# Loads of x.T and weights in another order, VectorE turns a second x.T tile, and the first normed x by rows and transposes

## The chip, the cores and the metric

The kernel runs on one core of a Trainium2 chip. The metric is the device time of one execution in microseconds (us). The engines of the core work side by side and wait for each other by semaphores: TensorE (PE in the profile, its weight loads PEld), VectorE (DVE), ScalarE (ACT), GpSimd (POOL) and SyncE (SP), whose queue issues nearly all DMAs here.

## The reference

Two transformer blocks in float32 over a sequence of 256 tokens of width 1024. What matters for the change is the first half layer:

```python
h = rmsnorm(x, norm_gain[0])                       # x * rsqrt(mean(x*x) + eps) * gain
qa, ka, va, qb, kb, vb, qm, gate = split_cols(h @ w_in_even[0], SPLIT_EVEN)
qa = rope_2d(rmsnorm(qa, q_norm_a), ...); ka = rope_2d(rmsnorm(ka, k_norm_a), ...)
ya, yb, ym = global_gqa(qa, ka, va), window_gqa(qb, kb, vb, ...), memory_attn(qm, mk, mv)
x = x + (concat(ya, yb, ym) * silu(gate)) @ w_out_even[0]
```

A second layer with neighborhood attention, a final norm, a hybrid mixer, a cross attention and an MLP follow; the change leaves them alone.

## The kernel before, in words

All products run on TensorE in float32r. Each operand is split into a high part, its value rounded to float32r, and a low part, the rest: three matmuls (high-high, high-low, low-high) give the product. A weight is loaded raw, ScalarE writes its high part (`t_wh`), VectorE its low part (`t_wl`; `split`, line 430). Raw weights have three buffers, the parts four each.

The work is not issued as written. Class `Plan` records every operation; `order` (line 162) then lays them out in time by a cost for each and a priority (place in the program, plus a bias), and the kernel is issued in the order that comes out. A DMA there takes its bytes over a rate, line 227. On the chip each engine runs its own stream strictly in that order.

The first half layer (`layer_even`, line 1008) starts before the norm's factor is known. x.T, the transposed input, is loaded in eight tiles of 128 features by `load_x` (line 392) and multiplied by the gain (`gain_t`, line 519; `t_gh`, high and low). For each of the eight weight tiles of 128 rows ("tile 0" to "tile 7"), `sweep` makes 12 matmuls with the columns of q, k and v of a and v of b (896 columns: 512 in two banks, 384 in two). Since the factor belongs to a token, it is multiplied in afterwards, on the results. The first x.T tile is turned by VectorE, the others by ScalarE.

The other projections want normed x.T. x itself is loaded by rows into two halves of 128 tokens, squared and summed; `rstd` makes the factor r on VectorE and GpSimd. `spread` (line 534) makes a diagonal of it and multiplies it with ones on TensorE, so that each partition holds all factors (`t_y`). Eight multiplies on VectorE (x.T times gain times spread factor, `t_xs`) and `hilo` give the high and low parts `t_hT`. Then come b's key (128 weight columns), the gates of a (two loads of 256 columns), mem-q (two loads), the keys and values of the memory, and so on. Beside them VectorE, ScalarE and GpSimd work on the rope of k and q, whose turned tiles go through TensorE transposes (`t_at<-t_cst,t_p`; `t_cst` holds the identity), and on the gain of the memory (`t_gh<-t_memT`).

Later norms of the kernel go by another way: x by rows times r (`t_xn`, `scaled`, line 644, on VectorE or ScalarE), 16 transposes of 128 x 128 on TensorE, and high and low parts out of PSUM with the gain (`t_mT`; `turns`, line 657).

Before the first data, 24 matmuls on zeros (`t_warm`) keep TensorE busy from 1.19 to 6.4 us.

Of the kernel before, what the change touches and what calls it, by code (L numbers as in the profile page):

```python
# [10 lines left out]
F32 = mybir.dt.float32  # L11
# [5 lines left out]
P = 128  # L17
# [12 lines left out]
class Plan:  # L30
# [131 lines left out]
    def order(self, prio):  # L162
# [37 lines left out]
        while len(seq) < n:  # L200
            best = None
            for e, c in cand.items():
                if not c:
                    continue
                t = max(avail[e][0], min(ready[i] for i in c))
                if best is None or t < best[0]:
                    best = (t, e)
            t, e = best
            c = cand[e]
            i = min((i for i in c if ready[i] <= t), key=lambda i: (prio[i], i))  # L210
            o = ops[i]
            for form in o["forms"]:
                cand[form[0]].remove(i)
            self.form[i] = next(f for f in o["forms"] if f[0] == e)
            start[i] = t
            self.held[i] = why[i] if ready[i] >= avail[e][0] else avail[e][1]
            end[i] = t + self.form[i][4]
            avail[e] = (end[i], i)
            done = end[i]
            if o["bytes"]:  # L220
                if e != "gpsimd":
                    ring[e] = max(ring[e], t) + 450.0
                    avail[e] = (ring[e], i)
                    bus = max(bus, ring[e] + 650.0)
                else:
                    bus = max(bus, end[i] + 650.0)
                bus += o["bytes"] / 358.0
                done = bus + o["after"]
            self.done[i] = done
            seq.append(i)  # L230
            for j, lat in self.next[i]:
                arrive(j, done + (lat if not o["bytes"] else 0.0), i)
            for name in o["uses"]:
                last[name] = max(last[name], (done + 190.0, i))
                left[name] -= 1
                if left[name] == 0:
                    k = self.key[name]
                    heapq.heappush(free[k], last[name] + (self.slot[name],))
                    give(k)
# [68 lines left out]
class Kernel:  # L308
# [59 lines left out]
    def consts(self):  # L368
# [9 lines left out]
        warm = self.base.tile([P, S], F32R, name="warm")  # L378
        nc.vector.memset(warm.bitcast(F32), 0.0)
        self.xT = [self.slot([P, 4, S], "xT", F32) for _ in range(2)]  # L380
        for k, queue in enumerate((nc.sync, nc.scalar)):
            self.load_x(k, 1, queue)
        busy = self.psum("at")
        for _ in range(WARM):
            nc.tensor.matmul(busy[:, 0, :], warm[:, :P], warm, start=True, stop=True)
# [133 lines left out]
    def gain_t(self, src, key, fast=False):  # L519

        nc = self.nc
        f = Halves(lambda: self.slot([P, 2, 2, S], "gh"))

        def turn(k):
            v, g, h, l = src[k // 4][:, k % 4, :], self.gcol(key, k), f(0, k), f(1, k)
            if k == 0 and fast:
                nc.vector.tensor_scalar(h, v, g, None, ALU.mult)
            else:
                nc.scalar.activation(h, v, AF.Copy, scale=g)
            nc.vector.scalar_tensor_tensor(l, v, g, h.bitcast(F32), ALU.mult, ALU.subtract)  # L530

        return f, turn
# [475 lines left out]
    def layer_even(self):  # L1008
# [5 lines left out]
        def columns(k0, parts, raw=None):  # L1014


            if raw is None:
                raw = self.wp.tile([P, 2, 896], F32, tag="raw", name=self.name("raw"), bufs=3)
            for j0, j1, d0, d1 in parts:
                c = d0 if d0 < 768 else d0 + 640  # L1020
                nc.sync.dma_start(raw[:, j0:j1, d0:d1], w_in[(k0 + j0) * P:(k0 + j1) * P, c:c + d1 - d0]
                                  .rearrange("(k p) c -> p k c", p=P))
            return raw
# [11 lines left out]
                             k == 0, k == KT - 1)  # L1035

        for k0 in range(0, KT, 2):
            raw = columns(k0, ((0, 1, 0, 512), (0, 2, 512, 768), (0, 2, 768, 896), (1, 2, 0, 512)) if k0 == 0 else
                          ((0, 2, 0, 768), (0, 2, 768, 896)) if k0 < 6 else ((0, 1, 0, 768), (0, 1, 768, 896)))
            if k0 < 6:  # L1040
                self.load_x(k0 + 2, 2, nc.sync)
            else:
                for t in range(2):
                    nc.ahead = True
                    nc.sync.dma_start(self.x[:, t, :], a["x"][0, t * P:(t + 1) * P])
                    nc.ahead = False
                columns(k0, ((1, 2, 0, 768), (1, 2, 768, 896)), raw)
# [8 lines left out]
        for c in range(2):  # L1056
            squares(c)
        r = self.rstd(ms)
        rb = self.spread(r, self.work("y", [P, S], YB))
        hT = Halves(lambda: self.slot([P, 2, 2, S], "hT"))  # L1060
        for c in range(2):
            t = self.slot([P, 4, S], "xs", F32)
            for k in range(4):
                nc.vector.scalar_tensor_tensor(t[:, k, :], self.xT[c][:, k, :], self.gcol("norm0", 4 * c + k), rb,
                                               ALU.mult, ALU.mult)
            for k in (0, 2):
                self.hilo(*hT.pair(4 * c + k), t[:, k:k + 2])
        nc.bias = 0
        self.sink = self.base.tile([P, 8], F32, name="sink")
        nc.sync.dma_start(self.sink, a["sink_b"].to_broadcast([P, 8]))  # L1070
# [488 lines left out]
```

## Time and profile before

| | |
|---|---|
| median of 3 runs | 773.08 us (772.73 to 773.56) |
| profiled execution | 773.77 us, its span 771.9 us |
| TensorE busy | 760.7 us, 99% of the span |
| VectorE, ScalarE busy | 614.3 us (80%), 529.0 us (69%) |
| chain that ended last | PE 82%, ACT 6%, DVE 6%, DMA 3% |
| granted TensorE clock | 0.997 of full speed over the span |

Matmuls overlap, and their ends are modelled, so a busy TensorE is one that had no long pause, and the pauses are found in the list of waits and in the timeline. All operations are recorded by one helper, so the line in most rows is L284; groups are told apart by tiles: `t_mm` and `t_at` are PSUM banks, `t_raw` a raw weight, `out<-in` says what is written from what. The queue of an engine, which issues its DMAs, has a q behind its name (SPq).

### The profile page before, as it was taken

Reading aid. Unit: us, or ns where it says so; the run is one execution under the profiler, and the core shown is the slowest. Engines: PE = TensorE matmul, PEld = TensorE weight load, DVE = VectorE, ACT = ScalarE, POOL = GpSimd, SP = SyncE. Lnnn points to the kernel's source line nnn. Section 1 sums busy time; section 2 is a strip of 40 time slices with the busy share of each in tenths; the row PEclk is TensorE's granted clock in tenths of the full one; section 3 lists DMA queues with packets and bytes.
Section 4 is the critical chain, followed back from the end, with each engine's and each line's share of the span. In section 5 each row is a group of like instructions: output and inputs, shape, how many; then the busy total and the mean of one; then the engine's idle time right before and its main releaser. Section 6 shows DMA issues by size and latency. Waiting matters only on the chain.

```text
span 771.9 us, 11841 instructions
## 1 busy us (share of the span) xinstructions
PE 760.7 (99%) x4370; PEld 662.6 (86%) x4370; DVE 614.3 (80%) x1136; ACT 529.0 (69%) x1034; POOL 66.6 (9%) x98
## 2 busy tenths in 40 slices
PE   9999999999999999999999999999999999999996
PEld 7898888888888888888888898899988888888885
DVE  5999998988779789979998899886677665555655
ACT  5687986976678678757796788466556765555562
POOL 2140010000001511132001000100000000000000
PEclk9999999999999999999999999999999999999998
DMA  8893555445568854765456644356535665656541
GB/s 315 284 268 111 165 183 177 159 165 164 164 211 250 218 188 144 199 197 193 134 191 194 191 163 156 117 165 219 191 110 164 195 188 167 204 177 209 170 163 55
DMA packets 109145, 140.39 MB, mean 182 GB/s; under 512 B 3744, under 2 KB 80736, under 8 KB 109088
## 3 DMA queue, kind: packets, MB, share of 16 engines
q1 hardware_dynamic: 103184, 131.12, 52.7%
q0 software_dynamic: 5472, 8.10, 4.8%
q8 instruction: 34, 0.56, 0.3%
q10 hardware_dynamic: 432, 0.43, 0.2%
q14 instruction: 23, 0.19, 0.1%
HBM read 134.92 MB, written 1.05 MB: 176 GB/s over the span
## 4 chain that ended last, share of the span: by engine, by line
PE 82%; ACT 6%; DVE 6%; DMA 3%; issue 2%; SPq 0%; POOLq 0%; POOL 0%; ACTq 0%; DVEq 0%
PE t_mm L284 61%; PE t_at L284 21%; DVE t_wl L284 2%; DMA t_raw<-in_w_in_even_dram 2%; ACT t_p L284 2%; ACT t_wh L284 2%; ACT t_y L284 1%; DVE t_y L284 1%; DVE t_p L284 1%; DMA t_xT<-in_x_t_dram 0%; ACT t_ph L284 0%; SPq L284 0%; ACT t_sum L284 0%; DVE t_pl L284 0%; DVE t_tanh L284 0%
## 5 line engine op out<-in xcount | busy, mean ns | idle before, releaser
L284 DVE TENSOR_TENSOR t_wl<-t_raw,t_wh 128x1024 fp32r<-128x1024 f32 (+2 forms) x238 | 288.7, 1217 | 69.9 <-ACT t_wh L284 67.2
L284 ACT ACTIVATE t_wh<-t_raw 128x1024 fp32r<-128x1024 f32 (+2 forms) x238 | 249.7, 1054 | 78.7 <-PE t_mm L284 57.4
L284 PE MATMUL t_mm<-t_mT,t_wh 128*128 128x512 f32 x496 | 179.6, 401 | 0.0
L284 PE MATMUL t_mm<-t_mT,t_wl 128*128 128x256 f32 x496 | 131.0, 283 | 0.0
L284 PE MATMUL t_mm<-t_wh,t_yh 128*128 128x512 f32 (+1 forms) x288 | 113.3, 393 | 0.0
L284 PE MATMUL t_mm<-t_wl,t_yh 128*128 128x512 f32 (+1 forms) x288 | 112.3, 390 | 0.0
L284 PE MATMUL t_mm<-t_wh,t_yl 128*128 128x512 f32 (+1 forms) x288 | 111.9, 391 | 0.0
L284 PEld LDWEIGHTS t_mm<-t_mT,t_wh 128*128 128x128 f32 x496 | 91.0, 188 | 13.4
L284 PEld LDWEIGHTS t_mm<-t_mT,t_wl 128*128 128x128 f32 x496 | 93.2, 189 | 6.6
L284 PE MATMUL t_at<-t_mT,t_wh 128*128 128x512 f32 x240 | 86.0, 395 | 0.0
L284 ACT COPY t_sum<-t_mm 128x256 f32<-128x256 f32 x90 | 33.2, 369 | 51.8 <-PE t_mm L284 51.3
L284 PE MATMUL t_mm<-t_wh,t_gh 128*128 128x256 f32 (+2 forms) x256 | 63.8, 333 | 0.0
L284 PEld LDWEIGHTS t_mm<-t_wl,t_yh 128*128 128x128 f32 x288 | 54.2, 188 | 10.7
L284 PEld LDWEIGHTS t_mm<-t_wh,t_yl 128*128 128x128 f32 x288 | 54.1, 188 | 10.6
L284 PEld LDWEIGHTS t_mm<-t_wh,t_yh 128*128 128x128 f32 x288 | 54.1, 188 | 10.3 <-ACT t_yh L284 0.3
L284 PE MATMUL t_at<-t_mT,t_wl 128*128 128x256 f32 x240 | 62.6, 280 | 0.0
L284 ACT ACTIVATE t_p<-t_p,t_st 128x256 f32<-128x256 f32 (+1 forms) x111 | 53.2, 494 | 10.6 <-DVE t_st L284 10.5
L284 PEld LDWEIGHTS t_at<-t_mT,t_wh 128*128 128x128 f32 x240 | 44.5, 188 | 8.3 <-issue 0.2
L284 DVE TENSOR_TENSOR t_sum<-t_mm,t_sum 128x256 f32<-128x256 f32 x90 | 37.9, 422 | 13.9 <-ACT t_sum L284 12.9
L284 PE MATMUL t_mm<-t_hT,t_wh 128*128 128x512 f32 (+1 forms) x160 | 48.3, 356 | 0.0
L284 PEld LDWEIGHTS t_at<-t_mT,t_wl 128*128 128x128 f32 x240 | 45.2, 188 | 3.5
L284 PE MATMUL t_mm<-t_gh,t_wh 128*128 128x512 f32 x128 | 47.3, 404 | 0.0
(189 smaller groups left out, 1371.7 us busy)
## 6 DMA issues: line engine op xcount, KB each, us to landing
t_raw<-in_w_in_odd_dram SPq DMA_DIRECT2D x20, 1024.0 KB, 5.2
t_raw<-in_w_up_dram SPq DMA_DIRECT2D x16, 1024.0 KB, 5.7
t_raw<-in_w_down_dram SPq DMA_DIRECT2D x16, 1024.0 KB, 5.0
t_raw<-in_w_in_dram SPq DMA_DIRECT2D x12, 1024.0 KB, 5.3
t_raw<-in_w_in_even_dram SPq DMA_DIRECT2D x10, 1024.0 KB, 5.1
t_raw<-in_w_mem_kv_dram SPq DMA_DIRECT2D x8, 1024.0 KB, 5.2
t_raw<-in_w_out_even_dram SPq DMA_DIRECT2D x6, 1024.0 KB, 5.2
t_raw<-in_w_out_odd_dram SPq DMA_DIRECT2D x6, 1024.0 KB, 5.9
```

Of the source, the lines that this page charges most:

```text
L284: f(*[self.real(v) for v in args], **{k: self.real(v) for k, v in kwargs.items()})
```

## The change

Five edits, all but the first in the first half layer:

- The planner's rate for DMAs goes from 358 to 320 bytes per ns. It is used for planning only.
- The second x.T tile is no longer loaded on ScalarE's queue at the start but on SP's, behind the first weights of q, k and v and ahead of tile 1's q columns.
- Tile 2 and tile 3 are loaded one after the other, tile 2's first 768 columns alone, instead of both in one DMA.
- VectorE, not ScalarE, multiplies the second x.T tile by the gain for its high part.
- The spread factor, the eight multiplies and the eight steps behind them are replaced by the later norms' way: `scaled` on the four quarters of x, 16 transposes and `turns`.

```diff
-                bus += o["bytes"] / 358.0
+                bus += o["bytes"] / 320.0
...
-        for k, queue in enumerate((nc.sync, nc.scalar)):
-            self.load_x(k, 1, queue)
+        self.load_x(0, 1, nc.sync)
...
-            if k == 0 and fast:
+            if k < 2 and fast:
                 nc.vector.tensor_scalar(h, v, g, None, ALU.mult)
...
-            for j0, j1, d0, d1 in parts:
+            for part in parts:
+                if len(part) == 2:
+                    self.load_x(*part, nc.sync)
+                    continue
+                j0, j1, d0, d1 = part
...
-            raw = columns(k0, ((0, 1, 0, 512), (0, 2, 512, 768), (0, 2, 768, 896), (1, 2, 0, 512)) if k0 == 0 else
-                          ((0, 2, 0, 768), (0, 2, 768, 896)) if k0 < 6 else ((0, 1, 0, 768), (0, 1, 768, 896)))
-            if k0 < 6:
-                self.load_x(k0 + 2, 2, nc.sync)
-            else:
+            raw = columns(k0, (((0, 1, 0, 512), (0, 2, 512, 768), (0, 2, 768, 896), (1, 1), (1, 2, 0, 512), (2, 2)),
+                               ((0, 1, 0, 768), (0, 2, 768, 896), (1, 2, 0, 768), (4, 2)),
+                               ((0, 2, 0, 768), (0, 2, 768, 896), (6, 2)),
+                               ((0, 1, 0, 768), (0, 1, 768, 896)))[k0 // 2])
+            if k0 == 6:
...
-        rb = self.spread(r, self.work("y", [P, S], YB))
-        hT = Halves(lambda: self.slot([P, 2, 2, S], "hT"))
+        halves = [self.slot([P, 2, 512], "xn", F32) for _ in range(2)]
         for c in range(2):
-            t = self.slot([P, 4, S], "xs", F32)
-            for k in range(4):
-                nc.vector.scalar_tensor_tensor(t[:, k, :], self.xT[c][:, k, :], self.gcol("norm0", 4 * c + k), rb,
-                                               ALU.mult, ALU.mult)
-            for k in (0, 2):
-                self.hilo(*hT.pair(4 * c + k), t[:, k:k + 2])
+            for t in range(2):
+                self.scaled(halves[c][:, t, :], self.x[:, t, c * 512:(c + 1) * 512], r[:, t:t + 1])
+        hT = self.turns("n", halves, "norm0")
+        self.flush("n")
```

The planner's order changes with it. On SP's queue, behind the loads of tiles 4 and 5 and of the last two x.T tiles, before (`t_raw_167` is tiles 6 and 7, `t_raw_216` b's key):

```order
L284 DMA t_x<-in_x_dram 128x1024 x2
L284 DMA t_raw_167<-in_w_in_even_dram 128x768
L284 DMA t_raw_167<-in_w_in_even_dram 128x128
L284 DMA t_raw_167<-in_w_in_even_dram 128x768
L284 DMA t_raw_167<-in_w_in_even_dram 128x128
L284 DMA t_raw_216<-in_w_in_even_dram 128x8x128
```

The same place of SP's queue now (`t_raw_171` is tiles 6 and 7):

```order
L284 DMA t_x<-in_x_dram 128x1024
L284 DMA t_raw_171<-in_w_in_even_dram 128x768
L284 DMA t_raw_171<-in_w_in_even_dram 128x128
L284 DMA t_x<-in_x_dram 128x1024
L284 DMA t_raw_171<-in_w_in_even_dram 128x768
L284 DMA t_raw_171<-in_w_in_even_dram 128x128
```

The second half of x has moved behind tile 6's two pieces.

On TensorE, the start of tile 4, before (`t_wh_228` and `t_wl_237` are its parts, `t_mm_146` to `t_mm_171` the four banks):

```order
L284 MATMUL t_mm_146<-t_wh_228,t_gh_197 128x512
L284 MATMUL t_mm_146<-t_wl_237,t_gh_197 128x512
L284 MATMUL t_mm_146<-t_wh_228,t_gh_197 128x512
L284 MATMUL t_mm_156<-t_wh_228,t_gh_197 128x512
L284 MATMUL t_mm_156<-t_wl_237,t_gh_197 128x512
```

The start of tile 4 on TensorE now (`t_wh_235`, `t_wl_244`):

```order
L284 MATMUL t_mm_144<-t_wh_235,t_gh_195 128x512
L284 MATMUL t_mm_152<-t_wh_235,t_gh_195 128x512
L284 MATMUL t_mm_161<-t_wh_235,t_gh_195 128x384
L284 MATMUL t_mm_168<-t_wh_235,t_gh_195 128x384
L284 MATMUL t_mm_144<-t_wl_244,t_gh_195 128x512
L284 MATMUL t_mm_144<-t_wh_235,t_gh_195 128x512
```

Three more high-part matmuls stand ahead of the first one with the low part.

On TensorE, inside tile 7, before (`t_wh_294` and `t_wl_304` are tile 7's parts, `t_at_335` is b's key, `t_at_354` the first gate with weights `t_wh_341`):

```order
L284 MATMUL t_mm_146<-t_wl_304,t_gh_242 128x512
L284 MATMUL t_at_335<-t_hT_324,t_wh_309 128x256
L284 MATMUL t_mm_146<-t_wh_294,t_gh_242 128x512
L284 MATMUL t_mm_156<-t_wh_294,t_gh_242 128x512
L284 MATMUL t_mm_156<-t_wl_304,t_gh_242 128x512
L284 MATMUL t_at_354<-t_hT_324,t_wh_341 128x256 x2
L284 MATMUL t_mm_156<-t_wh_294,t_gh_242 128x512
```

The end of tile 6 and the start of tile 7 on TensorE now (`t_wh_274`, `t_wl_281` are tile 6, `t_wh_301` tile 7, `t_xn` the scaled x):

```order
L284 MATMUL t_mm_168<-t_wh_274,t_gh_250 128x384
L284 MATMUL t_at_318<-t_cst,t_xn_306 128x128
L284 MATMUL t_at_320<-t_cst,t_xn_306 128x128
L284 MATMUL t_mm_168<-t_wl_281,t_gh_250 128x384
L284 MATMUL t_at_318<-t_cst,t_xn_306 128x128 x3
L284 MATMUL t_at_320<-t_cst,t_xn_306 128x128 x3
L284 MATMUL t_at_331<-t_cst,t_xn_311 128x128 x4
L284 MATMUL t_at_338<-t_cst,t_xn_311 128x128 x4
L284 MATMUL t_mm_168<-t_wh_274,t_gh_250 128x384
L284 MATMUL t_mm_144<-t_wh_301,t_gh_250 128x512
```

The transposes stand ahead of tile 7; the first matmul of a gate (`t_at_423`) now comes after the whole of b's key and two matmuls of tile 7.

On VectorE the first half of q in its rope (`t_p`) stood ahead of the low part of the second mem-q weights; now both low parts of these weights and two steps of the memory's gain stand ahead of it. Smaller moves of this kind go on up to about the 460th of some 3,900 rows of TensorE; behind it the streams are alike but for two short stretches on VectorE and ScalarE.

## Rows read from the trace of the kernel before

**Rows 1.** Busy us of each engine (instructions) in stretches; granted clock, DMA share, GB/s.
```profile
core 0: us, PE busy (x) PEld busy (x) DVE busy (x) ACT busy (x) POOL busy (x), PEclk, DMA share, GB/s
...
6.40:30.00 23.60, 21.49 (x104) 17.71 (x103) 17.65 (x32) 15.62 (x26) 4.89 (x13) 1.00 0.90 308
30.00:60.00 30.00, 29.33 (x239) 28.64 (x237) 29.48 (x67) 23.25 (x46) 10.86 (x13) 1.00 0.90 269
```

**Rows 2.** TensorE's waits: us in total, times, longest.
```profile
PE t_at L284 <- DVE t_p L284: 1.0, 2, 0.6
PE t_at L284 <- ACT t_wh L284: 0.9, 1, 0.9
PE t_mm L284 <- DVE t_wl L284: 0.9, 2, 0.6
```

**Rows 3.** Timeline of TensorE: start us, us, count; in brackets idle before, releaser.
```profile
9.18 0.40 PE L284 MATMUL t_mm<-t_wl,t_gh 128*128 128x512 f32 x1
9.42 0.62 PE L284 MATMUL t_mm<-t_wh,t_gh 128*128 128x512 f32 x2
...
12.65 0.50 PE L284 MATMUL t_mm<-t_wl,t_gh 128*128 128x512 f32 x1 [0.63 <-DVE t_wl L284]
...
17.79 0.50 PE L284 MATMUL t_mm<-t_wl,t_gh 128*128 128x512 f32 x1
...
21.77 0.71 PE L284 MATMUL t_at<-t_p,t_ones 128*128 128x128 f32 x4 [0.56 <-DVE t_p L284]
...
22.23 0.47 PE L284 MATMUL t_mm<-t_wl,t_gh 128*128 128x512 f32 x1
...
28.74 0.51 PE L284 MATMUL t_at<-t_hT,t_wh 128*128 128x256 f32 x2 [0.92 <-ACT t_wh L284]
...
44.02 0.33 PE L284 MATMUL t_at<-t_cst,t_p 128*128 128x128 f32 x1 [0.42 <-DVE t_p L284]
...
51.78 0.39 PE L284 MATMUL t_mm<-t_hT,t_wl 128*128 128x256 f32 x1 [0.25 <-DVE t_wl L284]
```

**Rows 4.** Timeline of ScalarE, from 15 to 29 us.
```profile
15.65 1.80 ACT L284 ACTIVATE t_wh<-t_raw 128x896 fp32r<-128x896 f32 x2 [2.55 <-DMA t_raw<-in_w_in_even_dram]
...
21.42 0.40 ACT L284 ACTIVATE t_p<-t_cst,t_rstd 128x128 f32<-128x128 f32 x1 [0.28 <-POOL t_rstd L284]
...
27.63 1.06 ACT L284 ACTIVATE t_wh<-t_raw 128x1024 fp32r<-128x1024 f32 x1 [1.59 <-DMA t_raw<-in_w_in_even_dram]
```

**Rows 5.** Timeline of SP's queue, the issuing of DMAs.
```profile
3.62 0.99 SPq L284 DMA_DIRECT2D t_raw<-in_w_in_even_dram  x2
...
6.99 1.18 SPq L284 DMA_DIRECT2D t_raw<-in_w_in_even_dram  x2
10.08 0.37 SPq L284 DMA_DIRECT2D t_xT<-in_x_t_dram  x1
10.50 1.07 SPq L284 DMA_DIRECT2D t_x<-in_x_dram  x2
```

**Rows 6.** DMA issues near 3.6 and 10.5: count, KB each, us to landing.
```profile
t_raw<-in_w_in_even_dram SPq DMA_DIRECT2D x1, 768.0 KB, 6.4
...
t_x<-in_x_dram SPq DMA_DIRECT2D x2, 512.0 KB, 7.4
```

**Rows 7.** Timeline of all engines at a later norm, 194.6 to 200 us.
```profile
194.64 1.28 DVE L284 TENSOR_SCALAR t_xn<-t_x,t_rstd 128x512 f32<-128x512 f32 x3 [0.84 <-POOL t_rstd L284]
...
195.70 1.69 PE L284 MATMUL t_at<-t_cst,t_xn 128*128 128x128 f32 x14
...
196.23 3.03 ACT L284 ACTIVATE t_mT<-t_at,t_gT 128x256 fp32r<-128x256 f32 x8 [0.65 <-PE t_at L284]
197.10 3.23 DVE L284 SCALAR_TENSOR_TENSOR t_mT<-t_at,t_gT,t_mT 128x256 fp32r<-128x256 f32 x8
197.15 0.71 PE L284 MATMUL t_mm<-t_wh,t_gh 128*128 128x512 f32 x2
```

**Rows 8.** Timeline of VectorE: first gate low part, rope tile of k.
```profile
31.41 1.22 DVE L284 TENSOR_TENSOR t_wl<-t_raw,t_wh 128x1024 fp32r<-128x1024 f32 x1
...
43.68 0.29 DVE L284 TENSOR_TENSOR t_p<-t_p,t_tanh 128x128 f32<-128x128 f32 x1
```

## The prediction

> **What bounds the kernel now.** I read the busy time by stretch first. Between 6.4 and 30 us TensorE is busy 21.49 of 23.60 us, at full clock; in the next 30 us it is busy 29.33 and VectorE 29.48 [rows 1]. The change sits in these two stretches. The list of TensorE's waits then holds five in them, 2.8 us together, and the timeline places them: at 12.65 and 51.78 for a low weight part that VectorE makes, at 21.77 for the diagonal of the spread factor, at 28.74 for a high weight part from ScalarE, at 44.02 for a rope tile [rows 2, 3]. A recorded wait is less than it costs: a 512-column matmul is listed 0.40 long, but the next one starts 0.24 after it [rows 3], so each wait costs its idle time plus about 0.16: 0.79, 0.41, 0.72, 1.08 and 0.58, together 3.6 us. Around them TensorE's matmuls stand end to end. So its stream sets the end: the change wins out of these 3.6 us and loses what it adds to the stream.
>
> Behind the waits stand the landings. ScalarE splits weights as they land, and starts at 15.65 on tiles 4 and 5 and at 27.63 on the first gate weights after standing for a DMA [rows 4]. SP's queue stood too: it issued nothing from 8.17 (6.99 + 1.18) to 10.08 [rows 5]; at 10.02 the 768 KB of tiles 2 and 3, issued at 3.62, had landed [rows 6]. By SP's list eight DMAs were then outstanding, and the ninth waited for the oldest.
>
> **The change part by part.**
>
> *Third weight tile alone.* Tiles 2 and 3 now land together at 10.02. With tile 2 by itself 384 KB fewer stand ahead of it, 1.3 us at 308 GB/s [rows 1]; the wait of 0.79 goes. What is late next is tile 4: the same bytes stand before it, so I let it land at 15.6 as now, and its low part comes at 17.7 again (the matmul on it now starts at 17.79 [rows 3]). TensorE has done more by then only because the planner now puts all four first high-part matmuls of tile 4 ahead of the first low-part one: three more, 0.24 + 2 x 0.18. Win 0.6, not 0.79.
>
> *Second x.T tile on SP's queue, turned by VectorE.* Tile 1's matmuls begin one weight tile after 6.4: from 12.65 to 17.79 two tiles pass [rows 3], so 2.5 us each, and 8.9. The x.T tile stands behind 640 KB of weights, and tile 1's weights behind it as before in bytes; both are there well before 8.9. First weights that land earlier bring nothing, as the warm-up matmuls hold TensorE until 6.4. Cost 0; the first tile's matmuls hide it, and without them it would be the transfer of 128 KB, 0.4 us.
>
> DMA: Bandwidth & Descriptors in the Trainium skill (Issuing engines are not separate DMA queues) says that issuing from several engines saves only the sequencer's issue time. By that the move from ScalarE's queue to SP's costs nothing; the pause at 8.17 [rows 5] shows that a DMA more on SP also takes one of eight places, and a later one waits for a landing: by the row this puts the last piece of tiles 4 and 5 back from 7.7 to the next landings, as an estimate by 0.9 us.
>
> *The norm.* Gone are the diagonal, its two ones-matmuls (four passes, 21.77 to 22.23: 0.46), their wait of 0.72, the copy, and the eight multiplies and eight hi/lo steps behind it. New are four scalings of x, 16 transposes, and eight hi and eight lo steps out of PSUM. The same step runs at 194.6 in this trace [rows 7]: 14 transposes from 195.70 to 197.15, 0.104 each, so 16 add 1.66; a scaling takes 0.43 on VectorE, the hi steps 0.38 on ScalarE, the lo steps 0.40 on VectorE.
>
> TensorE: Matmul & The Clock Gate in the Trainium skill (Part 4: PE-mode transpose) gives about 275 ns for one transpose inside a kernel. By that the 16 would add 4.4 instead of 1.66; the rows put two of them 0.104 apart [rows 7], so the measured distance stands.
>
> Does the norm come in time? The two loads of x, issued from 10.50, land 7.4 us later [rows 5, 6], the second near 18.5, and the factor is used at 21.42 [rows 4]. The second half of x now stands behind tile 6's 448 KB, 1.5 us at 308 GB/s: x at 20.0, factor at 22.9, scalings done by 24.3. TensorE reaches the first transpose with 8 + 12 + 10 matmuls of tiles 4 to 6 done after 17.7, 6.1 us: 23.8. The first two transposes need the first scaling only (23.4). No wait: 0, and up to 3 us if x came with the transfers behind it; I take 0, by the order of bytes. The low part of tile 7 stands behind two scalings on VectorE; it ends at 24.9, wanted at 26. Then ScalarE: key weights 1.06 to 25.4, eight hi steps 3.03 to 28.4, two v steps and a square about 1.0, gate weights 1.06 to 30.5; VectorE's low part, 1.22 [rows 8], ends at 31.7. TensorE, with transposes, tile 7 and 24 matmuls of b's key, is there at 31.5: wait 0.2.
>
> *The early gate matmuls.* Two of them stand inside tile 7 now and hold it for weights that land at 27.55: 1.08. In the new order they stand behind b's key projection; this goes.
>
> At this matmul on the first gate low part (now 32.77, as the low part ends at 31.41 + 1.22) the sum is 0.6 + 0.46 + 0.72 + 1.08 - 1.66 - 0.2 = 1.0.
>
> *What follows.* From the end of that low part VectorE works without a gap to the rope tile at 43.97, 11.3 us [rows 8]; one v step fewer stands in it, 0.3. So the tile comes at 42.7, TensorE at 43.44 - 1.0 = 42.4: wait 0.3 + 0.16 instead of 0.58, win 0.1. At 51.78 the low part of the second mem-q weights now stands ahead of q's rope on VectorE; that wait goes, 0.4. In turn q's rope and the memory keys come later against TensorE's order, and I charge 0.3 for waits between 55 and 61, where it has its closest starts; bounds 0 and the largest wait of the list, 0.92 + 0.16. The planner's bus rate costs nothing itself; from about 98 us on the streams are the same.
>
> Sum 1.0 + 0.1 + 0.4 - 0.3 = 1.2. The profiled execution took 773.77; 772.6 by the sum. The median of the runs is 0.69 below the profiled one, so 771.9.
>
> **The rivals.** About 0.2% (1.55 us) is what a measurement can tell here: faster is below 771.5, slower above 774.6.
>
> *All waits go* (VectorE and the landings keep ahead): 3.6 + 0.46 - 1.66 = 2.4, so 770.7. For it: tile 4 was issued early enough to land sooner if the pause on SP's queue shrinks. Against: its bytes.
>
> *VectorE decides, nothing won.* Between 30 and 60 us it is busy 29.48 of 30 [rows 1]; if its low parts come at the old times, TensorE's 1.0 lead at the gates is given back there: 773.0. Against it: it loses four 512-wide steps and gains two.
>
> *Slower: x lands late.* Place: the transposes, which stand in TensorE's queue ahead of all of tile 7, and behind them ScalarE's chain to the gate weights, which has no slack. Each us that x lands beyond 20 is lost one for one, after 0.4 at most. From 21.3 the kernel is slower than before; at 22.1, two more places lost on SP's queue, 774.0. For it: SP's pause; x's second half now waits behind two weight pieces and three DMAs more. Against: order of bytes.
>
> *Transposes one after the other.* If the 16 don't overlap, each takes its listed length, 0.33 for the one at 44.02 [rows 3]: 5.3 instead of 1.66, 3.6 us more, 775.5. Against it the 14 in 1.45 us [rows 7]. By the 275 ns of TensorE: Matmul & The Clock Gate in the Trainium skill (Part 4: PE-mode transpose) it would be 774.6.
>
> **How the numbers follow.** Forecast 771.9 (its own range 771.1 to 772.7) 0.43, of which two fifths below 771.5; all waits go 0.20; VectorE decides 0.14; x late 0.20, two fifths of it above 774.6; transposes 0.03, above. Faster 0.17 + 0.20 = 0.37; slower 0.08 + 0.03 = 0.11; within 0.52. The range 770.4 to 774.2 takes in the first three and half of x late.
>
> **What would show it.** Right: no wait near 12; tile 4's low part still at 17.7; 16 transposes within 2 us near 24 with no wait ahead of them; none for a high weight part near 28; the first gate low part's matmul near 31.7; one wait of a few tenths near 42.5 and none near 50. Wrong: a wait of more than half a us for a scaling or for x, a TensorE idle sum in the two stretches above 2.5 us, or tile 4 landing away from 15.6.

## The result and the profile after

The changed kernel took 774.94 us in the median of 14 runs (774.02 to 778.38), the kernel before 773.45 in the 14 runs beside them (772.25 to 774.82). The ratio is 1.0023, with a 95% interval of 1.0015 to 1.0032: a slowdown of 1.2 to 2.5 us, just outside the range and on the side that had the smallest chance. The profiled execution took 774.02, the shortest of the 14; its span is 772.2, against 771.9 in the profile of before.

The busy times by stretch, of after, in the columns of [rows 1]:

```profile
core 0: us, PE busy (x) PEld busy (x) DVE busy (x) ACT busy (x) POOL busy (x), PEclk, DMA share, GB/s
6.40:20.00 13.60, 13.13 (x65) 11.38 (x64) 9.81 (x17) 8.94 (x16) 3.67 (x12) 1.00 1.04 365
20.00:30.00 10.00, 10.00 (x65) 9.27 (x64) 8.11 (x17) 8.49 (x19) 0.71 (x1) 1.00 0.84 254
...
30.00:60.00 30.00, 28.34 (x228) 27.52 (x227) 28.36 (x66) 22.45 (x40) 13.21 (x13) 1.00 0.88 269
```

Up to 30 us TensorE is busier than before: 23.13 us of 23.60, where [rows 1] has 21.49. In the next 30 us it is the other way: 28.34 against 29.33, and VectorE 28.36 against 29.48. What the change won early was lost behind 30 us, and on both engines.

TensorE's timeline, to be read against [rows 3]:

```profile
9.91 0.49 PE L284 MATMUL t_mm<-t_wl,t_gh 128*128 128x512 f32 x1 [0.47 <-DVE t_wl L284]
...
12.44 0.40 PE L284 MATMUL t_mm<-t_wl,t_gh 128*128 128x512 f32 x1
...
17.90 0.40 PE L284 MATMUL t_mm<-t_wl,t_gh 128*128 128x512 f32 x1
...
24.05 0.38 PE L284 MATMUL t_at<-t_cst,t_xn 128*128 128x128 f32 x2
24.18 0.42 PE L284 MATMUL t_mm<-t_wl,t_gh 128*128 128x384 f32 x1
24.45 1.69 PE L284 MATMUL t_at<-t_cst,t_xn 128*128 128x128 f32 x14
...
30.93 0.34 PE L284 MATMUL t_mm<-t_wh,t_gh 128*128 128x384 f32 x1
31.11 0.34 PE L284 MATMUL t_mm<-t_wl,t_gh 128*128 128x384 f32 x1
31.28 0.28 PE L284 MATMUL t_at<-t_mT,t_wh 128*128 128x256 f32 x1
31.40 0.34 PE L284 MATMUL t_mm<-t_wh,t_gh 128*128 128x384 f32 x1
...
43.78 0.33 PE L284 MATMUL t_at<-t_cst,t_p 128*128 128x128 f32 x1 [1.50 <-DVE t_p L284]
```

The waits of [rows 3] at 12.65, 21.77, 28.74 and 51.78 are gone; two waits stand here. One is new, 0.47 at 9.91, for tile 1's low part. The other is at k's rope tile: 1.50 instead of 0.42, so that this transpose starts at 43.78, only 0.24 earlier than in [rows 3].

Tile 7's last three matmuls, 384 columns each, run from 30.93, behind the whole of b's key; the first matmul of the gate, at 31.28, stands between them. They finish the bank from which the second half of v is read, and here is what waited for it on VectorE:

```profile
22.61 0.88 DVE L284 TENSOR_SCALAR t_xn<-t_x,t_rstd 128x512 f32<-128x512 f32 x2 [0.89 <-POOL t_rstd L284]
...
30.11 1.23 DVE L284 TENSOR_TENSOR t_wl<-t_raw,t_wh 128x1024 fp32r<-128x1024 f32 x1 [0.56 <-ACT t_wh L284]
...
33.69 0.35 DVE L284 SCALAR_TENSOR_TENSOR t_vg<-t_mm,t_rstd,t_vg 128x128 fp32r<-128x128 f32 x1 [0.76 <-ACT t_vg L284]
34.47 0.35 DVE L284 SCALAR_TENSOR_TENSOR t_vg<-t_mm,t_rstd,t_vg 128x128 fp32r<-128x128 f32 x1 [0.44 <-ACT t_tanh L284]
...
43.44 0.28 DVE L284 TENSOR_TENSOR t_p<-t_p,t_tanh 128x128 f32<-128x128 f32 x1
```

The first gate's low part ends at 31.34 (30.11 + 1.23), 1.29 before that of [rows 8]. But VectorE then stands twice at v's second half: 0.76 for ScalarE's high parts, begun only at 33.02, and 0.44 for a step of ScalarE (`t_tanh`) that had itself stood 0.42 for VectorE. The bank was finished at 31.74 (31.40 + 0.34); ScalarE was then on b's key (`t_ks`), and the next gate weights stood ahead of v in its order:

```profile
31.13 0.78 ACT L284 ACTIVATE t_ks<-t_at 64x256 fp32r<-64x256 f32 x2
31.94 1.06 ACT L284 ACTIVATE t_wh<-t_raw 128x1024 fp32r<-128x1024 f32 x1
33.02 0.63 ACT L284 ACTIVATE t_vg<-t_mm,t_rstd 128x128 fp32r<-128x128 f32 x2
34.07 0.37 ACT L284 ACTIVATE t_tanh<-t_mm,t_rstd 128x128 f32<-128x128 f32 x1 [0.42 <-DVE t_vg L284]
```

1.20 of the 1.29 is spent there, and k's rope tile comes 0.24 earlier than in [rows 8], 43.44 for 43.68.

For what follows I use one mark: the start of TensorE's first memory scores, the last place before the streams are alike. It is at 101.04 in this profile, 100.86 in that of before. Before and after:

```profile
100.86 0.28 PE L284 MATMUL t_at<-t_mk,t_qm 128*128 128x256 f32 x1
```

```profile
101.04 0.28 PE L284 MATMUL t_at<-t_mk,t_qm 128*128 128x256 f32 x1
```

### The profile page after: what moved, and what is told of

Its sections match the earlier page's. It is cut to its first block, busy times and chain, and to the rows that moved or that the text cites. A ratio compares the mean times of both kernels' runs of the same rounds, so it can differ in the third digit from the quotient of the medians.

```text
span 772.2 us, 11873 instructions
## 1 busy us (share of the span) xinstructions
PE 761.4 (99%) x4382; PEld 664.5 (86%) x4382; DVE 614.2 (80%) x1140; ACT 529.3 (69%) x1031; POOL 68.4 (9%) x98
## 4 chain that ended last, share of the span: by engine, by line
PE 87%; ACT 5%; DVE 5%; issue 1%; DMA 1%; SPq 0%; POOLq 0%; POOL 0%; DVEq 0%
PE t_mm L284 65%; PE t_at L284 22%; ACT t_p L284 2%; DVE t_wl L284 2%; ACT t_wh L284 2%; DVE t_p L284 1%; DMA t_raw<-in_w_in_even_dram 1%; ACT t_y L284 0%; DVE t_y L284 0%; ACT t_ph L284 0%; DVE t_tanh L284 0%; SPq L284 0%; ACT t_sum L284 0%; DVE t_pl L284 0%; ACT t_tanh L284 0%
## 5 line engine op out<-in xcount | busy, mean ns | idle before, releaser
L284 PE MATMUL t_mm<-t_mT,t_wh 128*128 128x512 f32 (+1 forms) x656 | 228.0, 390 | 0.0
L284 PE MATMUL t_mm<-t_mT,t_wl 128*128 128x256 f32 x624 | 166.0, 284 | 0.0
L284 PEld LDWEIGHTS t_mm<-t_mT,t_wh 128*128 128x128 f32 x656 | 119.0, 189 | 15.6
L284 PEld LDWEIGHTS t_mm<-t_mT,t_wl 128*128 128x128 f32 x624 | 117.4, 189 | 8.0
L284 PE MATMUL t_at<-t_mT,t_wh 128*128 128x512 f32 (+1 forms) x320 | 100.9, 368 | 0.0
L284 PE MATMUL t_at<-t_mT,t_wl 128*128 128x256 f32 x280 | 73.9, 280 | 0.0
L284 PEld LDWEIGHTS t_at<-t_mT,t_wh 128*128 128x128 f32 x320 | 57.1, 189 | 8.3 <-issue 0.2
L284 ACT ACTIVATE t_p<-t_p,t_st 128x256 f32<-128x256 f32 (+1 forms) x111 | 53.2, 494 | 10.7 <-DVE t_st L284 10.5
L284 PEld LDWEIGHTS t_at<-t_mT,t_wl 128*128 128x128 f32 x280 | 52.9, 189 | 3.5
L284 POOL TENSOR_TENSOR t_rstd<-t_rstd,t_mhalf 128x2 f32<-128x2 f32 (+1 forms) x12 | 11.4, 953 | 434.5 <-DVE t_rstd L284 434.5
```

Of the source, the lines that this page charges most:

```text
L284: f(*[self.real(v) for v in args], **{k: self.real(v) for k, v in kwargs.items()})
```

## The experiments

Each was timed in 10 to 12 comparable runs against the kernel before on the same chip, unless another number stands. "Key later" below is a bias of 40 in the plan on b's key projection; "the slot" is a buffer of its own, 4 KB a partition, for b's key weights, which otherwise take one of the three raw buffers.

**The changed kernel again** (no edit).

> The changed kernel itself once more, to see a second execution by its profile. The one profiled so far took 774.02, while the median of its runs is 774.94. Theory A (VectorE and ScalarE give the lead back): the time is again 774.2 to 775.2, the profile shows TensorE without a wait from 10 to 42 us, one wait of 1.3 to 1.7 us for k's rope tile near 43.8, and the rest of the loss as small waits between 56 and 95 us. Theory B (landings): the execution differs from the first one ahead of 42 us, by a wait of 0.5 us or more for x, a scaling or a weight part between 20 and 32 us, and the wait at the rope tile shrinks by as much.

774.56 against 773.47, a ratio of 1.0013 with an interval of [1.0004, 1.0022]. The same waits behind 30 us: 1.50 at 43.55, VectorE's 0.76 and 0.44 at 33.47 and 34.25; the mark at 100.79. These belong to the kernel, not to one execution. The wait for tile 1's low part does not: it is missing here.

**b's key later.**

```diff
-        kb = self.k_stack(self.proj_t(w_in, 1280, hT, P, tag="at"), 1)
+        nc.bias = 40
+        kbp = self.proj_t(w_in, 1280, hT, P, tag="at")
+        nc.bias = 0
+        kb = self.k_stack(kbp, 1)
```

> The changed kernel with a bias of 40 on the matmuls of b's key: the last three matmuls of weight tile 7 come 11 rows earlier on TensorE, so the last v steps are free 2.5 us earlier; VectorE's low part of the second gate piece and ScalarE's key steps swap places with neighbours, all else as in the changed kernel. Theory A: VectorE's two waits of 0.76 and 0.44 for ScalarE's v steps near 33 to 34.5 go, the rope tile of k comes at 42.5 to 42.9 instead of 43.44, TensorE's wait of 1.50 falls to 0.3 to 0.7, and the time falls by 0.7 to 1.2 us against the changed kernel, to 773.7 to 774.3. Theory B (landings decide, or what is won is given back between 50 and 95 us): within 0.3 us of the changed kernel.

775.14, 1.0021 [1.0012, 1.0029]: nothing won. VectorE's two waits for v are gone and the rope tile's transpose comes at 42.82. Behind it VectorE stands again, and TensorE waits at q's rope. VectorE and TensorE of this kernel:

```profile
45.30 0.88 DVE L284 TENSOR_TENSOR t_ks<-t_at,t_ks 64x256 fp32r<-64x256 f32 x2 [1.24 <-ACT t_ks L284]
```

```profile
56.55 0.41 PE L284 MATMUL t_at<-t_cst,t_p 128*128 128x128 f32 x2 [1.44 <-DVE t_p L284]
```

ScalarE came late to t_ks behind its step on the memory, which landed at 43.0. The wait moved from the rope of k to that of q.

**The new norm alone**, in the kernel before (`scaled`, `turns` and `flush` as in the diff of the change; loads as before).

> The kernel before with the new norm alone (scaled x, 16 transposes); loads, planner rate and VectorE's turning as before, both halves of x loaded together. Theory A: the waits for the low part of tile 2 and for the diagonal: the first stays (0.8), the second goes with its two passes (1.2), the transposes add 1.7; the lead is again given back at k's rope tile, and what comes after 45 us decides: 773.0 to 774.2, that is 0 to 0.8 above before. Theory B (the changed kernel loses by late landings of x): no loss here, at or below before, 772.4 to 773.4.

774.10, 1.0006 [0.9997, 1.0014]; the mark at 100.65. It waits at 12.78, 21.69 and 44.97 (0.63, 0.39, 0.66). The norm by itself neither wins nor loses what can be measured.

**The loads alone**: after, with the old norm put back.

> The changed kernel with the old norm (diagonal, spread factor, eight multiplies); all other edits stay, and x's second half still stands behind tile 6's weights. Theory A: tile 2's wait goes (0.6 won), the waits for the diagonal and a gate weight stay or move, k's rope tile still sets the pace at 44: 772.9 to 773.6, within 0.3 of before. Theory B: the factor is late with x, the wait for the diagonal grows by 1 us or more, and b's key and the gates with it: 773.8 to 775.

775.42, 1.0024 [1.0015, 1.0033]; the mark at 101.71. So the slowdown is in the loads and the order planned around them, not in the transposes. TensorE stands elsewhere than in after, though: 1.74 in four places from 28.27 to 32.09, 0.60 at 52.39, and only 0.41 at k's rope tile.

**The planner's rate, late and early.** In before, the new rate only behind 150 us of the plan, and in after the old one there:

```diff
-                bus += o["bytes"] / 358.0
+                bus += o["bytes"] / (358.0 if t < 150000.0 else 320.0)
...
-                bus += o["bytes"] / 320.0
+                bus += o["bytes"] / (320.0 if t < 150000.0 else 358.0)
```

> The kernel before with the planner's rate of 320 only from 150 us of the plan on: TensorE's, SP's and GpSimd's streams are those of before word for word, and only VectorE's and ScalarE's order between some 233 and 252 us (the second layer's memory, its gain and its key steps) is that of the changed kernel. Theory D (the rate's late reordering costs): 0.6 to 1.1 us above before, 774.1 to 774.6; in the profile GpSimd's loads for the window bias start some 0.8 us later against TensorE, and VectorE's steps beside GpSimd's between 264 and 282 us, or the transposes at 375 us, show a wait of 0.3 us or more. Theory E (all of the loss lies in the first 100 us): within 0.3 us of before.

> The changed kernel with the planner's rate back at 358 from 150 us of the plan on: all streams up to 230 us are the changed kernel's, the stretch from 233 to 252 us is that of the kernel before. Theory D: 0.6 to 1.1 us below the changed kernel, 773.6 to 774.2, within 0.7 of before. Theory E: as the changed kernel, 774.5 to 775.

773.41 against 773.46, 1.0001 [0.9992, 1.0010], and 775.21, 1.0025 [1.0016, 1.0034]. The late reordering costs nothing that can be measured; the loss sits before 150 us of the plan. The first of the two is also a second look at the first 230 us of before, and it lacks a wait. TensorE where [rows 3] has 0.92 at 28.74, and ScalarE's gate weights:

```profile
28.74 0.33 PE L284 MATMUL t_mm<-t_wl,t_gh 128*128 128x384 f32 x1
28.91 0.34 PE L284 MATMUL t_mm<-t_wh,t_gh 128*128 128x384 f32 x1
...
42.94 0.33 PE L284 MATMUL t_at<-t_cst,t_p 128*128 128x128 f32 x1 [0.42 <-DVE t_p L284]
```

```profile
26.35 2.01 ACT L284 ACTIVATE t_wh<-t_raw 128x1024 fp32r<-128x1024 f32 x2 [0.48 <-DMA t_raw<-in_w_in_even_dram]
```

The first gate weights are there at 26.3, not at the 27.6 of [rows 4]; the rope's transpose is at 42.94 and the mark at 100.22.

In the same way the second of the two is a third look at after's first 230 us. x lands 0.6 later in it than in after's own profile, the factor is used at 23.19 and the mark is at 101.27. ScalarE's step on x's second half, first in after, then here, and TensorE's rope transpose here:

```profile
19.73 0.63 ACT L284 ACTIVATE t_p<-t_x 128x512 f32<-128x512 f32 x1 [0.25 <-DMA t_x<-in_x_dram]
```

```profile
20.32 0.63 ACT L284 ACTIVATE t_p<-t_x 128x512 f32<-128x512 f32 x1 [0.27 <-DMA t_x<-in_x_dram]
```

```profile
44.02 0.33 PE L284 MATMUL t_at<-t_cst,t_p 128*128 128x128 f32 x1 [1.49 <-DVE t_p L284]
```

The other profiles with after's loads go with this one. Of nine, x lands at 19.3 and 19.7 in the two of after and at 20.1 to 20.5 in the seven others, where the factor is used at 22.99 to 23.41. So after's own profiles show its early part on the good side.

**The kernel before again** (no edit, one run).

> The kernel before once more, one look, to see a second execution of it. In the first one the first gate weights (1 MB, issued at 18.8) took 8.8 us to land, at 27.6, while in the nine other profiled kernels of this study such a load took 7.0 to 8.0. Theory G (that landing was a late one, and the wait of 1.08 at 28.74 that the prediction wanted to win does not stand in most executions): it lands at 26 to 26.6, there is no wait near 28.7, the rope tile of k comes near 43, and the first memory scores (t_mk,t_qm) start at 100.0 to 100.5 instead of 100.86. Rival: the wait stands again, as in the first execution.

773.32. Again no wait near 28.7; the rope's transpose at 43.02, the mark at 100.19. The wait of 0.92 in [rows 3] was one late landing: 8.8 us from issue, where the twelve other profiles without the slot (below) have 7.0 to 8.0 for this 1 MB.

**The old rate throughout**, in after (358 for 320). Both halves of x then stand behind tile 6's weights.

> The changed kernel with the planner's old rate of 358 throughout: loads of the first tiles and the new norm as in the changed kernel, but the plan puts both halves of x behind tile 6's weights and orders the rest up to 100 us differently; late stretch nearly as before. Theory D: about as the changed kernel with the old rate late, 773.4 to 774.3. Theory B (late x costs): both halves of x are late, TensorE waits 0.5 to 1.5 us for the scalings near 24 us, and the time is at or above the changed kernel's, 774.5 to 775.5.

776.48 (5 runs), 1.0046 [1.0032, 1.0060]. x lands at 20.1, TensorE waits 0.48 at 17.85, 0.30 for a scaling at 22.91, 1.82 at 44.94 and 1.84 at 58.38; the mark at 103.11. A worse place in SP's queue, and the order that the plan makes of it, costs 1.3 us more on the same chip (776.48 to the 775.21 above).

**No low part of v on VectorE** in after (GpSimd writes zeros there, so v is rounded).

```diff
-                self.hilo(v[:, k, :, 0, :], v[:, k, :, 1, :], src, r[:, k:k + 1])
+                nc.scalar.activation(v[:, k, :, 0, :], src, AF.Copy, scale=r[:, k:k + 1])
+                nc.gpsimd.memset(v[:, k, :, 1, :].bitcast(F32), 0.0)
```

> The changed kernel without the four v steps on VectorE: the low parts of v are set to zero by GpSimd early on (this leaves out v's low parts). Theory A (VectorE's chain from 31 to 57 us sets the pace): four steps of 0.27 and two waits of 0.76 and 0.44 leave the chain, the rope tile of k comes at 41.2 to 41.8, ahead of TensorE, q's rope 1.5 us earlier too; the waits of 1.66 at 43.8 and 0.31 at 56.1 go, and the time falls by 1.2 to 2.0, to 772.8 to 773.6. Rival: what is won at 43.8 is given back at q's rope near 56 us and at the head's steps near 60 and 90 us, as in the run with b's key later: within 0.5 us of the changed kernel.

774.98, 1.0019 [1.0010, 1.0028]. Four VectorE steps less, the rope's transpose at 42.60 with a wait of 0.30, and 1.37 given back at q's rope, at 55.23; the mark is at 100.85. Between the two VectorE stood 1.28 for ScalarE (43.23 and 45.11), which had stood 1.99 for the memory's landing at 41.3. Taking work off VectorE before 43 us is not enough, either.

**The slot**, in before, in after, and in after with b's key later.

```diff
-        raw = self.load(w, 0, KT, c0, n)
+        if n == P:
+            raw = self.slot([P, KT, P], "rk", F32)
+            self.nc.ahead = True
+            self.nc.sync.dma_start(raw, w[:, c0:c0 + n].rearrange("(k p) c -> p k c", p=P))
+            self.nc.ahead = False
+        else:
+            raw = self.load(w, 0, KT, c0, n)
```

> The kernel before with b's key weights loaded into a free 4 KB slot instead of one of the three raw buffers, so that the second gate weights are issued one buffer earlier (near 19 instead of 23.8 us). Theory F (landings, held by the three buffers, pace VectorE and ScalarE up to 46 us): the dip of the DMA traffic from 20 to 26 us fills, the second mem-q weights land 1.5 to 3 us earlier than 46.2, and the time falls by 0.4 to 1.2, to 772.3 to 773.1. Theory A (VectorE's own work paces it, 25.3 of 26 us between 31 and 57): within 0.3 us of before.

> The changed kernel with b's key weights in a free slot. Theory F: the second gate weights are issued near 19 instead of 24.5 us, memory and mem-q weights land 1.5 to 3 us earlier, TensorE's wait of 1.66 for k's rope tile shrinks to below 0.8 and the time falls by 0.7 to 1.5, to 773.2 to 774.1. Theory A: the wait for the rope tile stays at 1.4 to 1.8 since VectorE's two waits for the late v steps stay; within 0.3 us of the changed kernel, 774.4 to 775.

> The changed kernel with both: b's key weights in a free slot, and the bias of 40 that brings tile 7's last matmuls earlier. Theory F with A: VectorE's waits for the v steps go, and ScalarE's wait for the memory's transposed input (which held VectorE 1.24 us at 45.3 and gave the gain back at 56.5) goes too; waits near 43 and 56 below 0.5 each, 772.6 to 773.6, at or below before. Theory A alone: what is won at 43 is given back at 56 again, 774.5 to 775.2.

773.31, 0.9997 [0.9987, 1.0007]; 775.01, 1.0020 [1.0010, 1.0030]; 773.95, 1.0007 [0.9998, 1.0015]. Earlier loads alone do nothing in either kernel: in after the wait of 1.50 at the rope stays. With b's key later they do: 43.14 and no wait above 0.4 at q's rope, the mark at 100.40. So two things had to be mended at once, the late bank of v and the buffer behind it.

**From there, three versions**: without the low part of v as well (v rounded); with the second x.T tile back on ScalarE's queue; and before with the new norm, the slot and b's key later (bias 100).

```diff
-        self.load_x(0, 1, nc.sync)
+        for k, queue in enumerate((nc.sync, nc.scalar)):
+            self.load_x(k, 1, queue)
...
-            raw = columns(k0, (((0, 1, 0, 512), (0, 2, 512, 768), (0, 2, 768, 896), (1, 1), (1, 2, 0, 512), (2, 2)),
+            raw = columns(k0, (((0, 1, 0, 512), (0, 2, 512, 768), (0, 2, 768, 896), (1, 2, 0, 512), (2, 2)),
```

> The run with the free slot and b's key later, without the four v steps on VectorE (v's low parts are zeros written by GpSimd; this leaves v's low parts out). Theory A (VectorE's work sets the pace): 1.1 us of work less ahead of k's rope tile; the waits near 43 and 55.6 (0.64 and 0.41) go, the first memory scores start at 99.2 to 99.8 instead of 100.4, time 773.0 to 773.5. Rival: it is given back later again, 100.2 or more, 773.8 to 774.3.

> The run with the free slot and b's key later, with the second x.T tile loaded on ScalarE's queue at the start as in the kernel before. Theory H (the new place of that load costs a wait for tile 1's low part): no wait near 9.7 us, TensorE 0.4 to 0.7 us earlier at tile 2; but if VectorE sets the pace from 20 us on (theory A) the first memory scores start at 100.2 to 100.6 all the same and the time stays at 773.7 to 774.2. Without theory A the 0.5 would be kept: 773.2 to 773.6.

> The kernel before with the new norm, b's key weights in a free slot and a bias of 100 on b's key; loads and the planner's rate as before. Theory A: the new norm takes about 1 us of VectorE's work between 20 and 57 us; with the waits for gate weights (2.0 at 33) and for the v steps out of the way the first memory scores start at 99.5 to 100.2, time 772.6 to 773.4, at or just below before. Rival (the 16 transposes cost what they add): 100.4 or more, 773.7 to 774.4.

773.88, 1.0009 [0.9999, 1.0020]; 772.16, 0.9982 [0.9973, 0.9991]; 774.03, 1.0008 [0.9999, 1.0017]. In the first the mark is at 99.45, 0.95 earlier than with the low part of v, and the time is no better: what is ahead at the mark can be lost behind it. In the last TensorE waits 1.67 for q's rope at 50.76. The second is faster than both kernels. With the x.T tile off SP's queue the plan also puts both halves of x ahead of tile 6's weights. VectorE uses the factor at 21.98 instead of 22.61, and in the next 36 us it stands twice:

```profile
21.98 0.88 DVE L284 TENSOR_SCALAR t_xn<-t_x,t_rstd 128x512 f32<-128x512 f32 x2 [0.88 <-POOL t_rstd L284]
...
24.19 1.09 DVE L284 TENSOR_TENSOR t_wl<-t_raw,t_wh 128x896 fp32r<-128x896 f32 x1 [0.33 <-ACT t_wh L284]
...
34.96 1.23 DVE L284 TENSOR_TENSOR t_wl<-t_raw,t_wh 128x1024 fp32r<-128x1024 f32 x1 [0.37 <-ACT t_wh L284]
```

The mark is at 99.15, 1.9 before after's.

**x ahead of tile 6, and the queue**, each by itself in after: a bias of -8 on the two loads of x; the x.T tile on ScalarE's queue, as in the diff above; and the bias with the slot and b's key later.

```diff
             if k0 == 6:
+                nc.bias = -8
                 for t in range(2):
...
+                nc.bias = 0
```

> The changed kernel with a bias of -8 on the two loads of x: both halves of x stand ahead of tile 6's weights on SP, as in the kernel before; by the plan that follows, tile 7's last three matmuls come right behind the first two of b's key. All other edits stay. Theory I (x's second half behind tile 6's weights delays the factor, and with it VectorE's whole chain to 57 us): the factor is used at 21.2 to 21.9 instead of 22.61, VectorE has no wait of 0.4 or more between 30 and 43, k's rope tile comes at 42.2 to 42.9, the first memory scores at 99.6 to 100.2, and the time falls by 1.0 to 1.8, to 772.9 to 773.8. Theory H (the second x.T load's place, tile 1's wait near 9.7, is the cause): within 0.4 of the changed kernel, 774.4 to 775.2.

> The changed kernel with the second x.T tile loaded on ScalarE's queue as in the kernel before; by the plan that follows, both halves of x stand ahead of tile 6 too. Theory I: as x_first, within 0.3 us of it, since VectorE's chain starts with the factor and not with tile 1. Theory H: 0.4 to 0.8 us below x_first.

> x_first with b's key weights in a free slot and the bias of 40 on b's key. Theory I: as slot_key_act, 771.9 to 772.5, faster than both kernels by 1 us or more, first memory scores at 99.0 to 99.5. Theory H: the gain of slot_key_act came from the x.T load: 773.2 or more.

774.48, 1.0008 [0.9999, 1.0017]; 773.21, 0.9990 [0.9981, 0.9999]; 772.44, 0.9981 [0.9973, 0.9990]. The marks are at 100.14, 99.44 and 99.44. In the first two the plan also moves tile 7's last matmuls back up, behind the first two of b's key. The first of the three, TensorE and then VectorE:

```profile
28.81 0.40 PE L284 MATMUL t_at<-t_mT,t_wh 128*128 128x256 f32 x2
29.04 0.34 PE L284 MATMUL t_mm<-t_wh,t_gh 128*128 128x384 f32 x1
29.22 0.34 PE L284 MATMUL t_mm<-t_wl,t_gh 128*128 128x384 f32 x1
29.39 0.33 PE L284 MATMUL t_mm<-t_wh,t_gh 128*128 128x384 f32 x1
```

```profile
22.55 0.88 DVE L284 TENSOR_SCALAR t_xn<-t_x,t_rstd 128x512 f32<-128x512 f32 x2 [0.89 <-POOL t_rstd L284]
...
31.18 1.12 DVE L284 SCALAR_TENSOR_TENSOR t_vg<-t_mm,t_rstd,t_vg 128x128 fp32r<-128x128 f32 x4
32.21 1.22 DVE L284 TENSOR_TENSOR t_wl<-t_raw,t_wh 128x1024 fp32r<-128x1024 f32 x1
```

v's four steps follow without a gap. The factor is used at 22.55, no earlier than in after's own profile, but earlier than in the seven other profiles with after's loads (22.99 to 23.41). So what this version wins over after, 0.4 to 1.3 us by the ratios, can come from the place of tile 7's matmuls, from the earlier x or from both.

The first two versions differ, up to 109 us, in nothing but the x.T tile's load and the place of two VectorE steps on that tile: 774.48 with the load on SP's queue, 773.21 on ScalarE's, 1.3 us. The third and the one at 772.16 differ in the same things alone and stand at 0.9981 and 0.9982: there the queue is worth nothing that can be measured. The third differs from the slot with b's key later in x's place and the order that the plan makes of it: 0.9981 against 1.0007, 2.0 us, with the factor at 22.26 instead of 23.31. The third and the one at 772.16 beat the kernel before by 1.4 to 1.5 us; the x.T tile on ScalarE's queue alone is 0.7 below it, with an interval that just clears 1.

## Why the prediction was wrong, step by step

**Third weight tile alone, win 0.6: right.** The wait near 12 is gone and the first matmul on tile 4's low part is at 17.90, forecast unchanged from 17.79.

**The x.T tile on SP, cost 0: wrong.** I held the landing of tile 1's weights against the time when TensorE wants them, "well before 8.9", and left out what stands between. ScalarE and VectorE of after:

```profile
7.78 0.95 ACT L284 ACTIVATE t_wh<-t_raw 128x896 fp32r<-128x896 f32 x1 [1.31 <-DMA t_raw<-in_w_in_even_dram]
```

```profile
6.50 0.35 DVE L284 TENSOR_SCALAR t_gh<-t_xT,t_gT 128x256 fp32r<-128x256 f32 x1 [0.68 <-DMA t_xT<-in_x_t_dram]
...
8.77 1.09 DVE L284 TENSOR_TENSOR t_wl<-t_raw,t_wh 128x896 fp32r<-128x896 f32 x1 [1.05 <-ACT t_wh L284]
```

The weights land at 7.78, the two steps of the split take 2.1, and the low part is there at 9.86; in before VectorE began it at 7.56. The wait is 0.63 by the rule of 0.16, but it is no fixed price: two of the eight other profiles with these loads have none, the rest an idle time of 0.39 to 0.63 at that place. With the edit undone VectorE begins at 7.73 and TensorE does not wait there. I also had an estimate of 0.9 for the place lost on SP's queue and charged nothing for it: the last piece of tiles 4 and 5 was issued at 9.50 instead of 7.70. What the queue costs is 1.3 us in one pair of versions and nothing in the other. DMA: Bandwidth & Descriptors in the Trainium skill (Issuing engines are not separate DMA queues) says that a second issuing engine saves only issue time. By that the move should cost the issue, listed 0.47 on SP's queue; the first pair has more, the second agrees. What in the move costs the 1.3 us, the landing near 7.8 or the places in SP's queue, no run separates.

**The norm: right in size and time.** 14 transposes take 1.69 and TensorE waits for no scaling. x lands near 19.7 (forecast 20.0), the factor is used at 22.61 (22.9), the first transpose is at 24.05 (23.8), the gate's low part ends at 31.34 (31.7). At 42 us TensorE is 1.3 ahead of the profile of before; the sum had 1.0. In the other executions with these loads x and the factor come up to 0.8 later, still without a wait for a scaling.

**The early gate matmuls, win 1.08: wrong.** It was read from one profile, and two other executions of before's early part do not have it. Worse, it was very likely counted twice. That wait puts the mark of this profile 0.64 to 0.67 later than in the two others (100.86 against 100.22 and 100.19), and its time lay 0.69 above the median of the runs shown. I won 1.08 against the profile and then took off the 0.69 as well. That the 0.69 is this wait is not shown: the spans of the two others are 771.8 and 771.5, against 771.9.

**What follows, "VectorE works without a gap": wrong, and the main one.** The sum had a wait of 0.3 at k's rope tile; it is 1.50. I carried the 11.3 us between the low part and the rope tile of [rows 8] over and took off a v step. But the change's own order had moved tile 7's last three matmuls behind b's key, and v's second half with them. From 31.34 to the end of the rope tile at 43.72 it took 12.4 instead of 11.0, of which 1.20 are the two waits at v. TensorE's lead over the profile of before falls from 1.3 at 42 us to 0.24 at 43.78, and at the mark it is 0.18 behind. Where this was relieved (b's key later, no low part of v) the gain was given back at q's rope, 1.37 to 1.44: VectorE stood 1.2 to 1.3 for ScalarE, which stood for the memory's landing, and had no idle time left to catch up in. This is near the rival "VectorE decides, nothing won", but not by its condition: the first low part came 1.29 early, and the lead was lost behind it. Its 773.0 rests on the same 0.69. Against the ordinary executions of before, the rope's transpose is 0.8 late (43.78 to 42.94 and 43.02), and the mark 0.8 (101.04 to 100.2), 0.6 in the changed kernel's second execution.

**Waits between 55 and 61, 0.3:** TensorE stood 0.15 at 56.13 and 0.5 in all at two places behind 80; the size was about right.

**The other rivals.** *All waits go*: four of five did (one of them, at 28.74, stands in one execution of before alone), the fifth grew, and one at tile 1 came. *x lands late*: in after's profiles it did not, by its own bound of 20; in the seven others with these loads it landed 0.1 to 0.5 beyond. TensorE never stood at the place that the rival names, the transposes, but VectorE's work starts with the factor, and x's place was worth 2.0 us in the versions with the slot. *Transposes one after the other*: refuted by the 14 in 1.69.

**The signs.** None of the three signs of being wrong came: no wait for a scaling, 2.1 us of TensorE idle in the two stretches, tile 4 split from 15.35. None of them looked at VectorE; of the signs of being right the one wait of a few tenths near 42.5 failed.

**Open.** The three marks of after (100.79, 101.04, 101.27) lie 0.6 to 1.1 behind the ordinary ones of before; the medians lie 1.1 to 1.75 apart. The rest falls behind 100 us, where the streams are alike. From the mark to the end of the span it takes 671.0 to 671.6 in the three profiles with before's early part and 671.2 to 671.9 in the three with after's; over all 20 profiles it is 670.9 to 672.7. Short waits of TensorE near 281 us (last section), 375 and 508 come and go; the one near 281 is in none of these six profiles. I have not shown that the change makes them more frequent. How much of the loss is v's late bank, how much x's late place, and how much the x.T tile's queue is open too: the plan moves other operations with each of them.

## What to carry to other kernels

A wait for a landing in a single profile is a sample: before counting its end as a win, see whether a second execution has it, and never take off the distance to the median beside it. Where a second engine is as busy as the first, follow that engine's chain through the new order, and look up when each of its inputs is finished there; a lead of TensorE is lost at the next tile that engine makes. A weight is ready when its split is, so a landing is compared with its use only with those steps added.

## What was not expected of the hardware

The same 1 MB load, the first gate weights, took 7.0 to 8.8 us from issue to landing in the profiles without the slot. And beside GpSimd VectorE can slow down: in the version with b's key later a 128x1024 low part took 1.95 us, at a place where the profiles of before and after have 1.21, while GpSimd ran a tensor operation across its start. GpSimd and VectorE of that version:

```profile
277.27 3.25 POOL L284 TENSOR_TENSOR t_rpbe<-t_cst,t_rpbraw 128x384 f32<-128x384 f32 x3
...
279.64 1.95 DVE L284 TENSOR_TENSOR t_wl<-t_raw,t_wh 128x1024 fp32r<-128x1024 f32 x1
```

In all 20 profiles such a low part took 1.20 to 1.23 us where no tensor operation of GpSimd overlapped it, and 1.21 to 2.04 where one did; most of these took 1.22 as well, so the overlap alone does not tell which are slow. In the seven profiles where the low part at this place took 1.95 or 1.96, TensorE stood 0.24 to 0.67 soon behind it (0.57 at 282.31 in the one shown); in the other 13 it did not.
